# A hybrid encoder's mixers: large elementwise work leaves GpSimd for VectorE and ScalarE

## The chip, the cores and the metric

The kernel runs on one core of a Trainium2 chip. A core has TensorE (PE, matrix products into PSUM), VectorE (DVE), ScalarE (ACT, functions and scaled copies), GpSimd (POOL) and SyncE (SP), which here only issues transfers. Each engine works through its own queue in order; semaphores order them against each other. The metric is the device time of one execution in microseconds.

## The reference, cut to what matters

Two layers over 256 tokens of 1024 features, all in float32. Each layer is: half a SwiGLU feed-forward step, a mixer, half a SwiGLU step.

```python
x = x + 0.5 * swiglu_ffn(x, ffn1_norm[l], ffn1_wi[l], ffn1_wo[l])
h = rmsnorm(x, mix_norm[l])
(a_q, a_k, a_v, sc_u, c_qlat, c_kvlat, c_krope, lru_u, gate_lin) = jnp.split(h @ w_in[l], split_idx, axis=-1)
o_a = gqa_mixer(...)          # 8 heads, softmax over 256 keys
o_b = shortconv_mixer(...)    # B * conv3(C * x)
o_c = mla_mixer(...)          # 8 heads from low-rank latents
o_d = rglru_mixer(...)        # gelu(gate) * (recurrence forwards + backwards)
y = jnp.einsum('bsnc,ncd->bsnd', branches, w_branch[l])
x = x + jnp.sum(sigmoid(gate_lin) * y, axis=2) @ w_out[l]
x = x + 0.5 * swiglu_ffn(x, ffn2_norm[l], ffn2_wi[l], ffn2_wo[l])
```

In the recurrence the decay is a = exp(-y) with y = 8 softplus(-lambda) r, and the input is scaled by sqrt(1 - a^2).

## The kernel before, in words

Every matrix product is made in float32r with both operands split in two parts that sum to them: `mm` (lines 208 to 212) issues high x high, low x high and high x low. So each weight that comes from memory is split on the chip: `Weights.split` (line 100) copies a unit of up to 1024 columns into a high part on ScalarE (line 110) and takes the difference, the low part, on VectorE (line 113). In some stretches every `share`-th low part is made on GpSimd (line 112): every fourth one from the mixer's first slot to the slot of the recurrence's output, every one from the last head's slot until the output projection. `AHEAD` = 2 units are split ahead of the one in use; four buffers hold high parts and four low parts.

A feed-forward step (`ffn`, line 382) is a long run of products of 128 features x 256 tokens with little else.

The mixer (line 475) first makes the latents and the queries, keys and values token by token, then runs a list of slots (line 905). A slot has an attention head or none, products that keep PE fed, and other work. For a head, `scores` and `exps` (line 445) make the scores, the row maxima on VectorE (line 448), a bias (line 450) and on ScalarE the exponentials with their row sums (line 454). `normalise` (line 459) takes the reciprocal and scales the probabilities on VectorE (line 462). One or two slots later `probs_t` (line 464) transposes them on PE and splits the result (`split`, lines 217 and 218), and `head_values` (line 952) multiplies them with the values (line 966), copies one half to the other half's partitions (line 968), adds (line 969) and splits the sum.

Beside this run: the scaling of the latents by their norm on VectorE (`lat_scale`, line 548); the width-4 and width-3 convolutions, all taps on VectorE (lines 649 and 652, 762 and 765); the recurrence's gates, decay (`lru_decay`, line 695: argument on VectorE, one exponential and one tanh of 1024 columns on ScalarE), roots (`lru_root`, line 705: a square root on ScalarE, then three GpSimd products or sums for each direction), scans on VectorE (line 719), closing sum and product on GpSimd (lines 722 and 723); the gelu (lines 665 to 672); the squares of the MLA norms on GpSimd (lines 803 and 808); and for each branch the gated up-projection, whose running sum is on GpSimd (line 880). The last branch's sum is on VectorE (lines 1008 and 1009), followed by the split of the merged features (line 1011, whose parts are `mgh` and `mgl`) and the output projection `pw`.

The order of the instructions on each engine isn't that of the program: a planner of the language lays it out when the kernel is built, with a simulated timeline of its own, so a change of engines can move instructions that the diff doesn't touch.

Of the kernel before, what the change touches and what calls it, by code (L numbers as in the profile page):

```python
# [15 lines left out]
DEPTH = 2  # L16
D = 1024
T = 256
# [10 lines left out]
# columns of the combined input projection  # L29
# [11 lines left out]
# per-layer columns of the packed per-channel parameters  # L41
# [7 lines left out]
# per-layer columns of the packed row vectors, then the rotary tables  # L49
# [7 lines left out]
# the first transfers of weights hold one unit each; so many of them go ahead of the constants  # L57
FIRST = 7
EARLY = 10
# GQA heads between a head's scores and its use  # L60
LAG = 2
# opening work in order: operand pair of x's tile k (k), split of the next weights (-1), square of tile k (10 + k)
# [3 lines left out]
class Weights:  # L66
    """Streams the weights in the order of their use and hands out each piece as two float32r
    parts that sum to it. Without the packed array it only records that order."""
# [3 lines left out]
    def __init__(self, nc, flat=None, order=None, raw_pool=None, hi_pool=None, lo_pool=None):  # L72
        self.nc, self.flat = nc, flat
        self.raw_pool, self.hi_pool, self.lo_pool = raw_pool, hi_pool, lo_pool
        self.recording = order is None
        self.order = [] if self.recording else order
        self.chunks = [] if self.recording else chunks_of(order)
        self.spare = None  # where the first transfers go
        self.share, self.n = 0, 0  # every share-th low part on GpSimd
        self.ci, self.off, self.loaded, self.ready, self.now = 0, 0, [], [], []  # L80
# [19 lines left out]
    def split(self):  # L100
# [10 lines left out]
        self.n += 1  # L111
        eng = self.nc.gpsimd if self.share and self.n % self.share == 0 else self.nc.vector
        b = eng.tensor_tensor(lo[:, :w], src, hi[:, :w].bitcast(F32), op=ALU.subtract)  # L113
# [20 lines left out]
def chunks_of(order):  # L134
    """Pieces grouped into split units of at most UNIT columns, those into transfers of MAXC."""
# [20 lines left out]
class Null:  # L156
    """Stands for every object of a trace that only records the order of the weights."""
# [18 lines left out]
def hybrid_encoder(ctx: ExitStack, tc: tile.TileContext, xT, par, rows, ident_d, flat, out, order=None):  # L176
# [31 lines left out]
    def mm(out, lhs, rhs, start, stop):  # L208
        """out (+)= lhs.T @ rhs, each operand a (high, low) pair of float32r."""
# [4 lines left out]
    def split(hi, lo, src, scale=None):  # L214
        """hi + lo = src (times a per-partition or constant scale)."""
# [9 lines left out]
    ones = const.tile([P, 1], F32, name="ones")  # L225
    V.memset(ones, 1.0)
    # brings ScalarE's function table on chip before the first data
# [24 lines left out]
    chp = const.tile([P, DEPTH, 8], F32, name="chp")  # L252
    hba = const.tile([P, DEPTH, 16], F32, name="hba")
    gqk = const.tile([P, DEPTH], F32, name="gqk")

    def prepare_parameters():
# [10 lines left out]
        # 4 softplus(-lam): log1p(exp(-|lam|)) by its series in z / (2 + z)  # L267
# [14 lines left out]
        V.tensor_scalar(chp, acc, 2.0, None, op0=ALU.mult)  # L282

# [3 lines left out]
    def rope_tables(l):  # L287
        """cos * gain and sin * (gain of the partner) for GQA q, k and MLA q, k."""
# [16 lines left out]
    def rope_swap(tmp, src, tabs, b, heads, d):  # L305
        """tmp = sin terms: the partners of src [P, heads, d] times sin * gain."""
# [12 lines left out]
    class Norm:  # L319
        """Operand pairs of x * gain as x's tiles become final, and the 1/rms they still lack."""  # L320
# [21 lines left out]
        def scale(self):  # L342
            """1/rms of every token, on the tokens' partitions."""
# [10 lines left out]
        def scale_rows(self):  # L354
            """The same as a row on all partitions."""
# [12 lines left out]
    def group(dst, name, l, kts, c0, pairs):  # L368
        """dst [128 features, T] = sum over k of W[k, c0:c0+128].T @ pairs[k]."""
# [3 lines left out]
    def groups(dsts, name, l, kts, c0s, pairs, late):  # L373
        """The same for several targets; the last `late` operands are left to the end."""
# [70 lines left out]
    def exps(pS, scl):  # L445
        """scl: per block [P, 1] scale of the scores."""
# [12 lines left out]
    def normalise(pe, sm):  # L459
        V.reciprocal(sm, sm)  # L460
        for b in range(2):
            V.tensor_scalar(pe[:, b, :], pe[:, b, :], sm[:, b : b + 1], None, op0=ALU.mult)
# [12 lines left out]
    def mixer(l, nrm, tabs, nxt):  # L475
        def tok_group(c0, width, wname, pairs, kts):
            """Token-major products of one column range, one bank per token block."""
# [15 lines left out]
        # latents, queries, keys and values, token-major  # L493
# [6 lines left out]
        # the function table of the attention and the gates, ahead of their need  # L500
# [4 lines left out]
        # fully normalised operand for the feature-major projections  # L505
# [19 lines left out]
        # norms of the latents  # L525
# [19 lines left out]
        def lat_scale():  # L545
            for b in range(2):
                for i, (o, w) in enumerate(spans):
                    V.tensor_scalar(lat[b][:, o : o + w], lat[b][:, o : o + w], lrs[:, b, i : i + 1], None, op0=ALU.mult)

        # transposed latents  # L550
# [13 lines left out]
        # GQA norms, rotary and operands  # L564
# [68 lines left out]
        # RG-LRU: width-4 convolution, gates, recurrences in both directions  # L633
# [11 lines left out]
        def lru_taps(p):  # L645
            for n in (2 * p, 2 * p + 1):
                src = lr["pad"][:, n, :]
                acc = lr["xc"][:, n * T : (n + 1) * T]
                V.tensor_scalar(acc, src[:, 0:T], col(l, O_LCW + n), col(l, O_LCB + n), op0=ALU.mult, op1=ALU.add)
# [11 lines left out]
        def gelu_gate():  # L661
            """2 gelu(gate) = gate * (1 + tanh(sqrt(2/pi) * (gate + 0.044715 gate^3)))."""
# [3 lines left out]
            V.tensor_scalar(gl, gl, 0.044715, 1.0, op0=ALU.mult, op1=ALU.add)  # L666
            G.tensor_tensor(gl, gl, lg, op=ALU.mult)

        def gelu_tanh():
            lg, gl = lr["g"], lr["gelu"]  # L670
            A.activation(gl, gl, AF.Tanh, scale=math.sqrt(2.0 / math.pi))
# [23 lines left out]
        def lru_decay(d):  # L695
            """a = exp(-y) and tanh(y / 2) for y = 8 softplus(-lambda) r; i * x."""
            r3 = th_r[d].rearrange("p (n t) -> p n t", t=T)
            c3 = chp[:, l, d * 4 : d * 4 + 4].unsqueeze(2).to_broadcast([P, 4, T])
            V.scalar_tensor_tensor(r3, r3, 1.0, c3, op0=ALU.add, op1=ALU.mult)
            dec[d] = m4("dec")  # L700
            A.activation(dec[d], th_r[d], AF.Exp, scale=-2.0)
            A.activation(th_r[d], th_r[d], AF.Tanh)
            V.scalar_tensor_tensor(th_i[d], th_i[d], 1.0, lr["xc"], op0=ALU.add, op1=ALU.mult)

        def lru_root():
            """sqrt(1 - a^2) = (1 + a) sqrt(tanh(y / 2)), quartered for i's and gelu's tanh forms."""
            A.activation(lr["r"], lr["r"], AF.Sqrt, scale=0.0625)
            for d in range(2):
                G.tensor_tensor(th_i[d], th_i[d], th_r[d], op=ALU.mult)
                G.tensor_tensor(th_r[d], th_i[d], dec[d], op=ALU.mult)  # L710
                G.tensor_tensor(th_i[d], th_i[d], th_r[d], op=ALU.add)
# [9 lines left out]
        def lru_add():  # L721
            G.tensor_tensor(th_r[0], th_r[0], th_r[1], op=ALU.add)
            G.tensor_tensor(th_r[0], th_r[0], lr["gelu"], op=ALU.mult)
# [14 lines left out]
        # short convolution  # L738
# [6 lines left out]
        def sc_x(p, pb):  # L745
# [12 lines left out]
            for j in range(2):  # L758
# [3 lines left out]
                V.tensor_scalar(acc, src[:, 0:T], col(l, O_SCW + n), col(l, O_SCB + n), op0=ALU.mult, op1=ALU.add)  # L762
# [10 lines left out]
        # MLA: up-projections, norms, rotary and operands  # L773
# [25 lines left out]
        def mla_square(which):  # L799
            for b in range(2):  # L800
                if which == 0:
                    sq = m3("sqm", cols=768)
                    G.tensor_tensor(sq, ml["qm"][b], ml["qm"][b], op=ALU.mult)
                    sq = sq.rearrange("p (h d) -> p h d", d=MD)
                else:
                    sq = m3("sqm", cols=512).rearrange("p (h d) -> p h d", d=HD)
                    kn = ml["kv3"][b][:, :, 0:64]
                    G.tensor_tensor(sq, kn, kn, op=ALU.mult)
# [36 lines left out]
        def mla_transpose(g, which):  # L845
            """Feature-major operand pair of heads 4g..4g+3."""
# [12 lines left out]
        # branch gates, up-projections and their gated sum  # L859
# [10 lines left out]
        def up(b, p, name):  # L870
            def done(p, pb):
# [6 lines left out]
                else:  # L878
                    V.scalar_tensor_tensor(t, t, 1.0, pb, op0=ALU.add, op1=ALU.mult)
                    G.tensor_tensor(mgp[p], mgp[p], t, op=ALU.add)  # L880
# [266 lines left out]
```

## Time and profile before

| what | us |
|---|---|
| median of 3 runs | 1418.28 (1417.96 to 1418.98) |
| span of the profiled execution, first to last instruction | 1416.7 |
| PE busy in that span | 1377.8 |
| VectorE busy | 999.4 |
| ScalarE busy | 746.0 |
| GpSimd busy | 247.0 |

For the profiled execution no time beside its span is listed; the median is 1.6 us above the span. The busy time of PE is the time in which a matmul or transposition was running, by modelled ends, so it contains slow ones too. The mixers lie between about 200 and 515 us and between about 905 and 1215 us; the rest is feed-forward.

### The profile page before, as it was taken

How to read it: one execution, taken by the hardware profiler on the slowest of the kernel's cores; microseconds unless marked ns; L12 is line 12 of the kernel's file. 1: busy time of each engine (PE TensorE's matmuls, PEld its weight loads, DVE VectorE, ACT ScalarE, POOL GpSimd, SP SyncE). 2: the span in 40 equal slices, each digit the busy share in tenths (PEclk: the TensorE clock that was granted, in tenths of full speed). 3: DMA queues.
4: the chain of work that ended last, by engine and by line, in shares of the span. 5: the costliest groups of instructions: out<-in, count | busy, mean ns of one | idle time of the engine just before them, and what ended most of it. 6: DMA issues, size and time to landing. Idle time of an engine off the chain costs nothing.

```text
span 1416.7 us, 26507 instructions
## 1 busy us (share of the span) xinstructions
PE 1377.8 (97%) x11184; PEld 1364.5 (96%) x11184; DVE 999.4 (71%) x1334; ACT 746.0 (53%) x1104; POOL 247.0 (17%) x199
## 2 busy tenths in 40 slices
PE   8999999997999999999999999999989999999999
PEld 8999999897899999999999999999889999999999
DVE  6666558989877676666566665599899777666653
ACT  6444447584556555444444444566745564554432
POOL 3200004329610400000000000032456104000000
PEclk9999999999999999999999999999999999999999
DMA  7555545433454355555555555444325534555552
GB/s 280 184 187 191 183 152 202 149 120 129 155 179 149 120 180 188 193 184 179 183 180 194 188 179 180 163 176 165 118 108 183 197 127 149 179 179 181 186 206 76
DMA packets 35831, 240.81 MB, mean 170 GB/s; under 512 B 3968, under 2 KB 5376, under 8 KB 9472
## 3 DMA queue, kind: packets, MB, share of 16 engines
q1 hardware_dynamic: 35712, 239.12, 47.6%
q8 instruction: 87, 1.43, 0.4%
q14 instruction: 32, 0.26, 0.1%
HBM read 238.06 MB, written 1.05 MB: 169 GB/s over the span
## 4 chain that ended last, share of the span: by engine, by line
PE 88%; DVE 5%; issue 2%; POOL 2%; ACT 1%; DMA 0%; SPq 0%; DVEq 0%; POOLq 0%; ACTq 0%
PE pg L211 6%; PE pu L211 6%; PE pg L212 6%; PE pg L210 6%; PE pu L212 6%; PE pu L210 6%; PE po L211 6%; PE po L210 6%; PE po L212 6%; PE pgt L210 4%; PE pgt L211 3%; PE pgt L212 3%; PE pa L211 2%; PE pa L212 2%; PE pa L210 2%
## 5 line engine op out<-in xcount | busy, mean ns | idle before, releaser
L110 ACT CAST hi<-raw 128x1024 fp32r<-128x1024 f32 (+4 forms) x459 | 474.2, 1035 | 500.5 <-PE po L211 117.0
L113 DVE TENSOR_TENSOR lo<-raw,hi 128x1024 fp32r<-128x1024 f32 (+4 forms) x428 | 539.5, 1261 | 276.1 <-ACT hi L110 274.5
L210 PE MATMUL pg<-xh,hi 128*128 128x256 f32 x704 | 199.0, 283 | 6.1 <-ACT hi L110 6.1
L211 PE MATMUL pg<-xl,hi 128*128 128x256 f32 x704 | 199.5, 283 | 0.0
L212 PE MATMUL pg<-xh,lo 128*128 128x256 f32 x704 | 199.2, 283 | 0.0
L211 PE MATMUL pu<-xl,hi 128*128 128x256 f32 x704 | 198.8, 282 | 0.0
L210 PE MATMUL pu<-xh,hi 128*128 128x256 f32 x704 | 198.4, 282 | 0.0
L212 PE MATMUL pu<-xh,lo 128*128 128x256 f32 x704 | 198.3, 282 | 0.0
L211 PE MATMUL po<-hl,hi 128*128 128x256 f32 x704 | 198.0, 281 | 0.0
L212 PE MATMUL po<-hh,lo 128*128 128x256 f32 x704 | 197.7, 281 | 0.0
L210 PE MATMUL po<-hh,hi 128*128 128x256 f32 x704 | 197.7, 281 | 0.0
L210 PE MATMUL pgt<-xnh,hi 128*128 128x256 f32 x512 | 146.4, 286 | 0.0
L212 PE MATMUL pgt<-xnh,lo 128*128 128x256 f32 x512 | 145.0, 283 | 0.7 <-DVE lo L113 0.7
L211 PE MATMUL pgt<-xnl,hi 128*128 128x256 f32 x512 | 145.5, 284 | 0.0
L210 PEld LDWEIGHTS pg<-xh,hi 128*128 128x128 f32 x704 | 133.8, 190 | 6.4 <-ACT hi L110 6.4
L212 PEld LDWEIGHTS pg<-xh,lo 128*128 128x128 f32 x704 | 133.8, 190 | 0.2 <-DVE lo L113 0.2
L211 PEld LDWEIGHTS pg<-xl,hi 128*128 128x128 f32 x704 | 133.8, 190 | 0.0
L212 PEld LDWEIGHTS pu<-xh,lo 128*128 128x128 f32 x704 | 133.1, 189 | 0.2 <-DVE lo L113 0.2
L211 PEld LDWEIGHTS pu<-xl,hi 128*128 128x128 f32 x704 | 133.2, 189 | 0.0
L210 PEld LDWEIGHTS pu<-xh,hi 128*128 128x128 f32 x704 | 133.0, 189 | 0.0
L211 PEld LDWEIGHTS po<-hl,hi 128*128 128x128 f32 x704 | 132.7, 188 | 0.0
L212 PEld LDWEIGHTS po<-hh,lo 128*128 128x128 f32 x704 | 132.6, 188 | 0.0
(301 smaller groups left out, 3052.7 us busy)
## 6 DMA issues: line engine op xcount, KB each, us to landing
raw<-weights SPq DMA_DIRECT2D x205, 1024.0 KB, 4.8
raw<-weights SPq DMA_DIRECT2D x9, 768.0 KB, 4.3
raw<-weights SPq DMA_DIRECT2D x4, 896.0 KB, 4.6
raw<-weights SPq DMA_DIRECT2D x3, 1008.0 KB, 4.7
raw<-weights SPq DMA_DIRECT2D x5, 512.0 KB, 8.0
out<-xg SPq DMA_DIRECT2D x8, 128.0 KB, 2.1
raw<-weights SPq DMA_DIRECT2D x1, 1016.0 KB, 4.8
raw<-weights SPq DMA_DIRECT2D x1, 968.0 KB, 4.6
```

What stands on the lines that cost most here:

```text
L110: a = self.nc.scalar.copy(hi[:, :w], src)
L113: b = eng.tensor_tensor(lo[:, :w], src, hi[:, :w].bitcast(F32), op=ALU.subtract)
L210: TE.matmul(out, lhs[0], rhs[0], start=start, stop=False)
L211: TE.matmul(out, lhs[0], rhs[1], start=False, stop=False)
L212: TE.matmul(out, lhs[1], rhs[0], start=False, stop=stop)
```

## The change

Low parts of weights are made on VectorE only (`share` is gone). Probabilities and latents are scaled on ScalarE. The first tap of both convolutions, with its bias, is made on ScalarE. In the decay the addition of 1 and the factor of each channel move into scale and bias of ScalarE's exponential and tanh, which are now issued for each 256 columns; a second small constant `chn` holds the factor of the exponential. The gelu's polynomial is one VectorE instruction in place of one on VectorE and one on GpSimd. The roots are two VectorE instructions for each direction in place of three on GpSimd. Closing sum and product of the recurrence and the gated sums move to VectorE, the squares of the MLA norms to ScalarE. Comments are removed as well, which the cut leaves out.

```diff
-        self.n += 1
-        eng = self.nc.gpsimd if self.share and self.n % self.share == 0 else self.nc.vector
-        b = eng.tensor_tensor(lo[:, :w], src, hi[:, :w].bitcast(F32), op=ALU.subtract)
+        b = self.nc.vector.tensor_tensor(lo[:, :w], src, hi[:, :w].bitcast(F32), op=ALU.subtract)
...
+        V.tensor_scalar(chn, acc, -4.0, None, op0=ALU.mult)
...
-            V.tensor_scalar(pe[:, b, :], pe[:, b, :], sm[:, b : b + 1], None, op0=ALU.mult)
+            A.activation(pe[:, b, :], pe[:, b, :], AF.Copy, scale=sm[:, b : b + 1])
...
-                    V.tensor_scalar(lat[b][:, o : o + w], lat[b][:, o : o + w], lrs[:, b, i : i + 1], None, op0=ALU.mult)
+                    A.activation(lat[b][:, o : o + w], lat[b][:, o : o + w], AF.Copy, scale=lrs[:, b, i : i + 1])
...
-                V.tensor_scalar(acc, src[:, 0:T], col(l, O_LCW + n), col(l, O_LCB + n), op0=ALU.mult, op1=ALU.add)
+                A.activation(acc, src[:, 0:T], AF.Identity, scale=col(l, O_LCW + n), bias=col(l, O_LCB + n))
...
-            V.tensor_scalar(gl, gl, 0.044715, 1.0, op0=ALU.mult, op1=ALU.add)
-            G.tensor_tensor(gl, gl, lg, op=ALU.mult)
+            V.scalar_tensor_tensor(gl, gl, 1.0 / 0.044715, lg, op0=ALU.add, op1=ALU.mult)
...
-            A.activation(gl, gl, AF.Tanh, scale=math.sqrt(2.0 / math.pi))
+            A.activation(gl, gl, AF.Tanh, scale=0.044715 * math.sqrt(2.0 / math.pi))
...
-            V.scalar_tensor_tensor(r3, r3, 1.0, c3, op0=ALU.add, op1=ALU.mult)
             dec[d] = m4("dec")
-            A.activation(dec[d], th_r[d], AF.Exp, scale=-2.0)
-            A.activation(th_r[d], th_r[d], AF.Tanh)
+            for n in range(4):
+                sl, c = slice(n * T, (n + 1) * T), slice(d * 4 + n, d * 4 + n + 1)
+                A.activation(dec[d][:, sl], th_r[d][:, sl], AF.Exp, scale=chn[:, l, c], bias=chn[:, l, c])
+                A.activation(th_r[d][:, sl], th_r[d][:, sl], AF.Tanh, scale=chp[:, l, c], bias=chp[:, l, c])
...
-                G.tensor_tensor(th_i[d], th_i[d], th_r[d], op=ALU.mult)
-                G.tensor_tensor(th_r[d], th_i[d], dec[d], op=ALU.mult)
-                G.tensor_tensor(th_i[d], th_i[d], th_r[d], op=ALU.add)
+                V.scalar_tensor_tensor(th_r[d], dec[d], 1.0, th_r[d], op0=ALU.add, op1=ALU.mult)
+                V.tensor_tensor(th_i[d], th_i[d], th_r[d], op=ALU.mult)
...
-            G.tensor_tensor(th_r[0], th_r[0], th_r[1], op=ALU.add)
-            G.tensor_tensor(th_r[0], th_r[0], lr["gelu"], op=ALU.mult)
+            V.tensor_tensor(th_r[0], th_r[0], th_r[1], op=ALU.add)
+            V.tensor_tensor(th_r[0], th_r[0], lr["gelu"], op=ALU.mult)
...
-                V.tensor_scalar(acc, src[:, 0:T], col(l, O_SCW + n), col(l, O_SCB + n), op0=ALU.mult, op1=ALU.add)
+                A.activation(acc, src[:, 0:T], AF.Identity, scale=col(l, O_SCW + n), bias=col(l, O_SCB + n))
...
-                    G.tensor_tensor(sq, ml["qm"][b], ml["qm"][b], op=ALU.mult)
+                    A.square(sq, ml["qm"][b])
...
-                    G.tensor_tensor(sq, kn, kn, op=ALU.mult)
+                    A.square(sq, kn)
...
-                    G.tensor_tensor(mgp[p], mgp[p], t, op=ALU.add)
+                    V.tensor_tensor(mgp[p], mgp[p], t, op=ALU.add)
```

The calls of `share` in the slots and after the last branch are removed.

## Rows read from the trace of the kernel before

**Rows 1.** The page's first part: busy time, share of the span and instructions of each engine.

```profile
PE 1377.8 (97%) x11184; PEld 1364.5 (96%) x11184; DVE 999.4 (71%) x1334; ACT 746.0 (53%) x1104; POOL 247.0 (17%) x199
```

**Rows 2.** Windows: the stretch, its length, busy time (and instructions) of PE, weight loads, VectorE, ScalarE and GpSimd, the granted clock, the share and rate of transfers. A piece of the first mixer, the first mixer, the two feed-forward steps between, the second mixer.

```profile
300.00:375.00 75.00, 63.09 (x454) 59.88 (x454) 66.98 (x80) 45.07 (x75) 52.29 (x27) 0.93 0.34 119
222.00:515.00 293.00, 276.44 (x2184) 269.86 (x2183) 242.12 (x345) 171.56 (x293) 114.76 (x71) 0.98 0.42 150
515.00:923.00 408.00, 408.00 (x3400) 408.00 (x3400) 256.27 (x313) 198.53 (x257) 4.82 (x10) 1.00 0.52 184
923.00:1215.00 292.00, 278.89 (x2194) 273.13 (x2193) 244.66 (x352) 175.80 (x297) 101.72 (x54) 0.98 0.43 152
```

**Rows 3.** PE's waits over the whole span: which instructions waited for which, us in total, times, the longest.

```profile
PE pov L966 <- DVE pl L218: 13.0, 4, 4.5
PE pov L966 <- ACT ph L217: 6.4, 3, 3.1
PE pg L210 <- ACT hi L110: 6.1, 2, 4.6
PE pw L211 <- DVE mgl L221: 4.7, 2, 2.4
PE pa L211 <- POOL lo L113: 1.4, 1, 1.4
PE pkT L615 <- DVE ro L605: 1.3, 1, 1.3
```

**Rows 4.** Windows of 5 us in the columns of rows 2: beside the attention stalls (325, 330, 355, 1030, 1055 us) and behind the output projection's (500, 1200 us).

```profile
325.00:330.00 5.00, 1.49 (x7) 1.49 (x8) 4.93 (x6) 0.00 (x0) 5.00 (x3) 0.53 0.47 161
330.00:335.00 5.00, 5.00 (x33) 4.54 (x33) 4.83 (x7) 3.36 (x7) 3.35 (x1) 0.78 0.00 2
355.00:360.00 5.00, 3.62 (x14) 3.62 (x15) 3.44 (x6) 0.65 (x2) 0.12 (x1) 0.66 0.28 85
500.00:505.00 5.00, 5.00 (x33) 5.00 (x33) 2.66 (x6) 1.07 (x3) 0.00 (x0) 0.72 0.51 180
1030.00:1035.00 5.00, 3.44 (x17) 3.44 (x18) 4.76 (x8) 1.57 (x5) 3.01 (x2) 0.69 0.01 3
1055.00:1060.00 5.00, 4.69 (x19) 4.69 (x20) 4.97 (x5) 3.55 (x6) 2.72 (x2) 0.66 0.21 85
1200.00:1205.00 5.00, 4.99 (x23) 4.99 (x24) 3.19 (x7) 0.83 (x2) 0.00 (x0) 0.50 0.51 200
```

**Rows 5.** VectorE's timeline in the first mixer: start, duration (of all `xN` together), line, instruction, tiles, in brackets the idle time ahead of it.

```profile
304.30 0.61 DVE L462 TENSOR_SCALAR pe<-pe,sm 128x256 f32<-128x256 f32 x2
...
314.53 2.58 DVE L113 TENSOR_TENSOR lo<-raw,hi 128x1024 fp32r<-128x1024 f32 x1 [3.41 <-ACT hi L110]
...
317.24 4.69 DVE L462 TENSOR_SCALAR pe<-pe,sm 128x256 f32<-128x256 f32 x2
...
322.42 2.83 DVE L113 TENSOR_TENSOR lo<-raw,hi 128x1024 fp32r<-128x1024 f32 x1
325.17 2.57 DVE L218 TENSOR_TENSOR oal<-o,oah 128x256 fp32r<-128x256 f32 x1
327.77 0.69 DVE L218 TENSOR_TENSOR pl<-pT,ph 128x512 fp32r<-128x512 f32 x1
...
350.45 4.82 DVE L462 TENSOR_SCALAR pe<-pe,sm 128x256 f32<-128x256 f32 x2
```

**Rows 6.** GpSimd's timeline in the same stretch, in the same columns.

```profile
313.63 5.74 POOL L709 TENSOR_TENSOR thi<-thi,thr 128x1024 f32<-128x1024 f32 x2 [12.76 <-ACT thr L707]
319.30 2.48 POOL L710 TENSOR_TENSOR thr<-thi,dec 128x1024 f32<-128x1024 f32 x1
321.74 2.42 POOL L113 TENSOR_TENSOR lo<-raw,hi 128x1024 fp32r<-128x1024 f32 x1
...
327.40 5.95 POOL L711 TENSOR_TENSOR thi<-thi,thr 128x1024 f32<-128x1024 f32 x2
```

**Rows 7.** VectorE's instructions in groups of one line, shape and operation: count, busy us, mean ns, idle time before. In this order: the feed-forward stretch from 540 to 920 us (one row), the first mixer from 222 to 515 us (two rows), the second from 923 to 1215 us (three rows).

```profile
L113 DVE TENSOR_TENSOR lo<-raw,hi 128x1024 fp32r<-128x1024 f32 x124 | 151.7, 1224 | 104.1 <-ACT hi L110 104.1
...
L113 DVE TENSOR_TENSOR lo<-raw,hi 128x1024 fp32r<-128x1024 f32 x65 | 87.5, 1348 | 19.7 <-ACT hi L110 18.7
L462 DVE TENSOR_SCALAR pe<-pe,sm 128x256 f32<-128x256 f32 x32 | 20.8, 691 | 0.6
...
L113 DVE TENSOR_TENSOR lo<-raw,hi 128x1024 fp32r<-128x1024 f32 x65 | 90.0, 1389 | 21.3 <-ACT hi L110 20.7
L462 DVE TENSOR_SCALAR pe<-pe,sm 128x256 f32<-128x256 f32 x32 | 12.4, 431 | 0.6
L1009 DVE TENSOR_TENSOR mg<-mg,th 128x256 f32<-128x256 f32 x8 | 7.1, 909 | 0.0
```

**Rows 8.** GpSimd's groups over the whole span, in the columns of rows 7: low parts of weights, gated sums.

```profile
L113 POOL TENSOR_TENSOR lo<-raw,hi 128x1024 fp32r<-128x1024 f32 x28 | 70.1, 2506 | 165.5 <-ACT hi L110 164.9 <-PE pT L469 0.6
L880 POOL TENSOR_TENSOR mg<-mg,th 128x512 f32<-128x512 f32 x16 | 21.8, 1362 | 74.9 <-DVE th L879 74.9
```

**Rows 9.** ScalarE's groups over the whole span, in the columns of rows 7: the residual's scaling into its high part, the residual's square.

```profile
L220 ACT ACTIVATE xh<-xg,prm 128x256 fp32r<-128x256 f32 x40 | 20.2, 505 | 2.9 <-DVE xg L435 2.7 <-DVE xg L1021 0.2
...
L336 ACT ACTIVATE sq<-xg 128x256 f32<-128x256 f32 x42 | 16.4, 403 | 0.0
```

**Rows 10.** ScalarE's waits over the whole span, in the columns of rows 3.

```profile
ACT pe L454 <- DVE nb L450: 32.6, 11, 5.8
```

More of the change, by code (lines that the diff above doesn't have):

```diff
@@ L78, in __init__ @@
         self.spare = None
-        self.share, self.n = 0, 0
         self.ci, self.off, self.loaded, self.ready, self.now = 0, 0, [], [], []
@@ L252, in hybrid_encoder @@
     chp = const.tile([P, DEPTH, 8], F32, name="chp")
+    chn = const.tile([P, DEPTH, 8], F32, name="chn")
     hba = const.tile([P, DEPTH, 16], F32, name="hba")
@@ L695, in lru_decay @@
         def lru_decay(d):
-            r3 = th_r[d].rearrange("p (n t) -> p n t", t=T)
-            c3 = chp[:, l, d * 4 : d * 4 + 4].unsqueeze(2).to_broadcast([P, 4, T])
-            V.scalar_tensor_tensor(r3, r3, 1.0, c3, op0=ALU.add, op1=ALU.mult)
             dec[d] = m4("dec")
-            A.activation(dec[d], th_r[d], AF.Exp, scale=-2.0)
-            A.activation(th_r[d], th_r[d], AF.Tanh)
+            for n in range(4):
+                sl, c = slice(n * T, (n + 1) * T), slice(d * 4 + n, d * 4 + n + 1)
+                A.activation(dec[d][:, sl], th_r[d][:, sl], AF.Exp, scale=chn[:, l, c], bias=chn[:, l, c])
+                A.activation(th_r[d][:, sl], th_r[d][:, sl], AF.Tanh, scale=chp[:, l, c], bias=chp[:, l, c])
             V.scalar_tensor_tensor(th_i[d], th_i[d], 1.0, lr["xc"], op0=ALU.add, op1=ALU.mult)
@@ L899, in call @@
             return lambda: f(*args)
-        def share(n):
-            return lambda: setattr(W, "share", n)
         slots = [
-            (None, [proj("pxb", C_XB, 0, lru_conv)], [share(4), lat_norms, gqa_norms, lat_scale]),
+            (None, [proj("pxb", C_XB, 0, lru_conv)], [lat_norms, gqa_norms, lat_scale]),
             (None, [proj("pxb", C_XB, 1, lru_conv)], [lat_transpose, call(gqa_rotate, 0), call(gqa_rotate, 1), call(lru_taps, 0)]),
@@ L920, in mixer @@
             (None, [gate(1, 3), up(1, 3, "ob"), call(mla_up, 1, "kvup")], [lru_out, call(mla_square, 0)]),
-            (None, [gate(3, 0), up(3, 0, "od")], [share(0), call(mla_sum, 0), call(mla_swap, 0), call(mla_square, 1)]),
+            (None, [gate(3, 0), up(3, 0, "od")], [call(mla_sum, 0), call(mla_swap, 0), call(mla_square, 1)]),
             (None, [gate(3, 1), up(3, 1, "od")], [call(mla_sum, 1), call(mla_query, 0), call(mla_swap, 1), mla_values]),
@@ L931, in mixer @@
             (14, [gate(2, 2)], []),
-            (15, [gate(2, 3), share(1)], []),
+            (15, [gate(2, 3)], []),
             (None, [up(0, 2, "oa"), up(0, 3, "oa")], []),
@@ L1011, in mixer @@
             split(*merged[n], m, scale=0.5)
-        W.share = 0
         pws = [bank("pw")[:, :T] for _ in range(2)]
```

## The prediction

> **What bounds the kernel now.** I read the page's busy line first: PE is busy 1377.8 of 1416.7 us [rows 1]. So at most 38.9 us are idle time of PE, and no engine but PE can be the limit on the average; what the other engines can change is only when PE stands still. The windows by stage come next [rows 2]: in the feed-forward stretch from 515 to 923 us PE is busy 408.00 of 408.00 us with 3400 matmuls, 0.120 us each, and there the change touches nothing. The two mixers show the idle time: 293.0 - 276.4 = 16.6 us in the first and 292.0 - 278.9 = 13.1 us in the second, 29.7 us together. The rest (about 9 us) is the opening and the last store.
>
> PE's waits say where this lies [rows 3]. The values' matmuls of the attention heads wait 13.0 us for the low part of the transposed probabilities (VectorE) and 6.4 us for the high part (ScalarE); a low part of weights made on GpSimd costs 1.4 us: 20.8 us in the attention stretches (group A). The output projection waits 4.7 us for the merged branches (group B). The keys' transposition waits 1.3 us (group C).
>
> Behind the long waits the clock is down [rows 4]. Granted shares of 0.53, 0.78, 0.66, 0.69 and 0.66 stand in five windows of 5 us beside the attention stalls, 0.72 and 0.50 after the output projection's. A share below 1 is a mixture of the two levels, 1.2 and 2.4 GHz. What this cost is (1 - share) x PE busy: 0.70 + 1.10 + 1.23 + 1.07 + 1.59 = 5.7 us beside A, 1.40 + 2.50 = 3.9 us behind B.
>
> Why VectorE is late there is seen by laying its timeline over GpSimd's [rows 5, 6]. Two probability scalings take 0.61 us together at 304.30 us, and 4.69 us at 317.24 us; a low part of weights takes 2.58 and 2.83 us, a 128x256 low part 2.57 us. In just this time GpSimd runs without a gap from 313.6 to 333.4 us: the recurrence's products and one low part. The scalings end at 321.93 us, just after the GpSimd product that runs to 321.78; the low part begun at 322.42 ends at 325.25, 1.1 us (its own time) after the GpSimd low part that runs to 324.16. In the same time the probabilities' low part at 327.77 us, which reads one operand from PSUM, takes its normal 0.69 us beside a GpSimd product. I read this as two engines that can't both read two SBUF operands at once: one stands until the other's instruction is over. At 350.45 us the scalings again take 4.82 us. Behind both places stands a stall of PE of over 4 us (the longest of rows 3), because scaled probabilities, their transposition and the values' product follow each other.
>
> **The change, part by part.** *Off GpSimd:* the low parts of weights (28 of 1024 columns at 2.51 us, and three shorter ones), the gated sums (16 at 1.36 us) [rows 8], the recurrence's products (12, 2.5 to 3.0 us each [rows 6]), and 14 closing steps, gate products and squares of 1.4 to 3 us (an estimate from these rows by size). That is about 82 + 22 + 34 + 30 = 168 of 247 us [rows 1]. What is left is small: powers of row sums, the rotary swaps, memsets.
>
> *Onto VectorE:* an unhindered 1024-column instruction with two SBUF inputs takes 1.22 us [rows 7], one of 512 columns 0.69 us [rows 5]. Low parts of weights 31 x 1.22 = 38 us, gated sums 16 x 0.69 = 11 us, the roots' products 8 x 1.22 = 9.8 us (12 GpSimd instructions become 8 here), the two closing steps 4 x 1.22 = 4.9 us, the gate's fused step about 2 x 0.6 = 1.1 us: 65 us. *Off VectorE:* 64 probability scalings at 0.61 / 2 = 0.31 us [rows 5] = 20 us, the decay's argument 4 x 1.22 = 4.9 us, first taps and latents about 24 x 0.35 = 8.4 us (estimates from the scaling's 0.31 us): 33 us. Net + 32 us, 16 us for each mixer.
>
> Against it stands what VectorE loses now by standing. Its low parts of weights take 1348 and 1389 ns in the mixers and 1224 ns in the feed-forward stretch: 65 x 0.124 = 8.1 and 65 x 0.165 = 10.7 us. The scalings take 20.8 and 12.4 us where 32 x 0.31 = 9.9 us are due: 10.9 and 2.5 us. Eight sums of the second mixer's end take 7.1 us instead of 8 x 0.37 = 3.0: 4.1 us [rows 7]. So at least 19.0 and 17.3 us of standing go, against 16 us of work that comes: VectorE's sum hardly moves, 242 to 245 us a mixer [rows 2]. The gain isn't a lighter VectorE but that its instructions keep to their short times, and a chain of three of them no longer takes 10 us.
>
> *Onto ScalarE:* 64 scalings of 128x256, with a factor for each partition. The nearest rows are a square without such a factor, 403 ns, and the residual's scaling with one, 505 ns [rows 9]; I take the second, 64 x 0.505 = 32 us. 16 first taps at the same price 8 us, 8 latent scalings about 4 us, the decay in 32 pieces instead of 8 whole instructions about 5 us, eight squares of the MLA norms about 6 us (estimates from the same two rows by size): 55 us, some 27 us a mixer. ScalarE is at 171.6 and 175.8 of 293 us [rows 2], so this lies beside PE's work. On this the Trainium skill speaks against the move: "ScalarE: Activation LUTs", section "What ACT_TABLE_LOAD costs", says that an instruction without a pointer takes 186 ns and 0.833 ns an element, and that each pointer operand adds some 93 ns. By it a scaling would take an estimated 493 ns, 60% more than VectorE's 0.31 us; the trace agrees (505 ns). By the pointerless price the 64 would be 26 us; neither reaches PE.
>
> *A wait that is added:* on ScalarE the scaling stands behind VectorE's reciprocal of the row sums, which itself waits for ScalarE's exponentials. Queued behind it are the high parts of weights, and PE waits for those. What covers it is the lead of the weights: two units of 8 pieces with 3 matmuls each, 2 x 24 x 0.120 = 5.8 us. ScalarE already stands 32.6 us behind VectorE for the scores' bias, up to 5.8 us at a time [rows 10], and the only wait of PE for high parts of weights, 6.1 us [rows 3], is the opening's. I price the new wait at 0, with 32 x 1.5 us as the upper bound if the cover is gone (below).
>
> *The sum.* Group A 20.8 + 5.7 us, B 4.7 + 3.9 us, C 1.3 us: 36.4 us if everything goes. What stays: from 300 to 375 us VectorE is busy 67.0 of 75 us [rows 2]. Take off the stretch of rows 5: (2.58 - 1.22) + (4.69 - 0.61) + (2.83 - 1.22) + (2.57 - 0.41) + (4.82 - 0.61) = 13.4 us and five pairs of scalings, 3 us; add four low parts of weights 4.9, root products 4.9, closing steps 2.4, gate 0.6 = 12.8 us: 63 us of work, where PE's own need is 63.1 us less its slow-clock loss, about 60 us. VectorE is still full there, so a chain can still come late; I keep a third of A: 7 us idle and 2 us of clock. For B: the two sums and low parts of rows like those above get short, but two low parts of weights come onto VectorE in the same 10 us; I keep 1 us of idle and 1 us of clock. Gain 36.4 - 11 = 25.4 us. The profiled execution's span is 1416.7 us, 1.6 us below the median of 1418.28 us; the span's prediction is 1391.3 us, with the same 1.6 us around it 1393 us.
>
> **The rivals.** *Half comes back (1404 to 1414 us).* VectorE at 100% between 300 and 375 us, and at 1010 to 1060 us likewise, makes the attention chain late as before: only C, B and a third of A go, 1.3 + 6.6 + 8.8 = 16.7 us less, or 1401.6 us, and with new short waits for low parts of weights (31 more of them queue on VectorE, at an estimated 0.3 us each: 9 us) 1411 us. For it: the 63 against 60 us above. Against it: the standing I could take off came from a few rows alone, so the 63 us are an upper value.
>
> *No difference (within 0.2%).* The standing of VectorE isn't due to GpSimd's SBUF reads, so the times stay. Against it: the ends in rows 5 follow those in rows 6. The Trainium skill has this as a rule ("SBUF — State Buffer", section "Who interferes with whom"): a VectorE instruction with two SBUF inputs, or in a mode that uses both ports, and a GpSimd instruction that reads SBUF exclude each other, and the one that comes second stands for the whole of the first. By that rule this case wouldn't arise, and the trace agrees; the chance stays at 0.08 because the order of instructions on each engine is laid out anew by the planner when engines change, which no row of before shows.
>
> *Slower (1430 us).* The added wait decides. It stands in ScalarE's queue once a head. If VectorE's queue ahead of the reciprocal is over 5.8 us long when ScalarE gets there, the high parts behind come late; at an estimated 1.5 us of stall in each of the 32 heads this is 48 us, against the 36.4 us: 1418.3 - 36.4 + 48 = 1430 us. For it: ScalarE's waits for VectorE reach that length already [rows 10], where VectorE itself stood behind GpSimd. Against it: just this standing goes.
>
> **How the numbers follow.** The forecast (1380 to 1403 us) 0.63; half comes back 0.17; no difference 0.08; slower 0.12. About 0.2%, 2.8 us, is what a measurement of this kernel can tell from no change. So faster 0.80, same 0.08, slower 0.12. The low end is all of the 36.4 us gone, 1382 us, and some 2 us of PE's shorter waits that I gave no row; the high end reaches into the second case and leaves about 0.2 above it: 1412 us.
>
> **What would show it.** GpSimd's busy time near 80 us (247 - 168); PE's waits for the two parts of the probabilities under 8 us in total; no low part of weights over 1.5 us from 310 to 360 us; ScalarE's scaling at 0.40 to 0.51 us; the clock windows behind the attention stalls at 1.00. I am wrong if VectorE's instructions stay long without GpSimd, or if PE's waits turn to the high parts of weights behind ScalarE's scaling, or to low parts queued on VectorE.

## The result, and the profile after

The changed kernel takes 1385.96 us (median of 4 runs, 1385.48 to 1386.98) beside 1418.4 us for the kernel before: a ratio of 0.9771, 95% interval 0.9757 to 0.9785. The forecast was 1393 us with 1380 to 1412 as its range.

The page's first part (answers to [rows 1]):

```profile
PE 1367.8 (99%) x11184; PEld 1356.3 (98%) x11184; DVE 939.7 (68%) x1302; ACT 798.0 (58%) x1224; POOL 90.6 (7%) x126
```

Read it against PE first. The span went from 1416.7 to 1385.2 us, 31.5 us. PE has the same 11184 matmuls and is busy 10.0 us less. Of this 7.4 us is clock: (1 - share) x busy time, summed over all windows of 5 us, was 10.6 us and is 3.1 us. Its idle time fell from 38.9 to 17.4 us, 21.5 us. Then VectorE: it received work and is busy 59.7 us less. Windows by stage and of 5 us, in the columns of [rows 2] and [rows 4]:

```profile
300.00:375.00 75.00, 73.70 (x568) 71.02 (x567) 64.54 (x97) 60.80 (x102) 16.51 (x12) 1.00 0.45 161
222.00:505.00 283.00, 279.53 (x2247) 274.32 (x2246) 220.78 (x346) 202.65 (x361) 33.02 (x35) 0.99 0.46 161
505.00:910.00 405.00, 405.00 (x3364) 405.00 (x3362) 251.99 (x302) 197.09 (x256) 4.82 (x10) 1.00 0.52 183
910.00:1190.00 280.00, 275.52 (x2220) 270.25 (x2220) 216.07 (x341) 200.85 (x356) 26.90 (x17) 0.99 0.45 160
325.00:330.00 5.00, 5.00 (x38) 4.44 (x37) 5.00 (x9) 4.59 (x10) 0.00 (x0) 1.00 0.13 18
330.00:335.00 5.00, 5.00 (x43) 5.00 (x43) 5.00 (x10) 3.12 (x6) 0.00 (x0) 1.00 0.48 195
485.00:490.00 5.00, 5.00 (x32) 5.00 (x31) 2.08 (x5) 0.42 (x1) 0.00 (x0) 0.66 0.47 197
1170.00:1175.00 5.00, 4.17 (x22) 3.97 (x21) 2.32 (x7) 1.18 (x3) 0.00 (x0) 0.66 0.26 108
```

The gain lies in the mixers; the feed-forward stretch is as before. From 300 to 375 us PE ran 454 matmuls before and runs 568 now, while VectorE is about as busy (66.98 and 64.54 us) and GpSimd has dropped from 52.29 to 16.51 us. The clock is at 1.00 where the attention stalls had been, and at 0.66 in two windows only, both behind the output projection.

PE's waits (answers to [rows 3]):

```profile
PE pg L207 <- ACT hi L109: 5.8, 2, 4.8
PE pw L209 <- DVE lo L110: 2.4, 2, 1.3
PE pS L207 <- ACT qTh L214: 1.7, 2, 1.0
PE pa L208 <- DVE lo L110: 1.2, 1, 1.2
PE pov L959 <- ACT ph L214: 1.0, 1, 1.0
PE pw L208 <- DVE mgl L218: 1.0, 2, 0.8
...
PE pw L207 <- ACT mgh L217: 0.3, 1, 0.3
```

The 13.0 us for the probabilities' low part are gone, the 6.4 us for their high part are 1.0. What the output projection waits for has changed its name from the merged features to a low part of its weights (L110), and is hardly less: 2.4 + 1.0 + 0.3 us (L209, L208, L207) where there were 4.7 us for low parts and 0.6 us for a high part.

VectorE's timeline in the stretch of [rows 5]:

```profile
321.10 2.36 DVE L706 SCALAR_TENSOR_TENSOR thr<-dec,thr 128x1024 f32<-128x1024 f32 x2 [0.81 <-ACT thr L704]
323.49 0.69 DVE L215 TENSOR_TENSOR pl<-pT,ph 128x512 fp32r<-128x512 f32 x1
324.10 1.22 DVE L707 TENSOR_TENSOR thi<-thi,thr 128x1024 f32<-128x1024 f32 x1
325.23 1.22 DVE L110 TENSOR_TENSOR lo<-raw,hi 128x1024 fp32r<-128x1024 f32 x1
326.37 1.22 DVE L707 TENSOR_TENSOR thi<-thi,thr 128x1024 f32<-128x1024 f32 x1
327.50 0.42 DVE L215 TENSOR_TENSOR oal<-o,oah 128x256 fp32r<-128x256 f32 x1
```

A low part of weights takes 1.22 us here (2.58 and 2.83 before) and the 128x256 low part 0.42 us (2.57). The roots' products, 2.5 to 3.3 us each on GpSimd, take 1.2 us each. Groups of the whole span, ScalarE's scaling of the probabilities (answers to [rows 9]):

```profile
L461 ACT ACTIVATE pe<-pe,sm 128x256 f32<-128x256 f32 x64 | 29.4, 510 | 1.9 <-DVE sm L459 1.9
```

### The profile page after: what moved, and what is told of

It is laid out like the page before. It is cut to its first block, busy times and chain, and to the rows that moved or that the text cites. A ratio compares the mean times of both kernels' runs of the same rounds, so it can differ in the third digit from the quotient of the medians.

```text
span 1385.2 us, 26443 instructions
## 1 busy us (share of the span) xinstructions
PE 1367.8 (99%) x11184; PEld 1356.3 (98%) x11184; DVE 939.7 (68%) x1302; ACT 798.0 (58%) x1224; POOL 90.6 (7%) x126
## 5 line engine op out<-in xcount | busy, mean ns | idle before, releaser
L110 DVE TENSOR_TENSOR lo<-raw,hi 128x1024 fp32r<-128x1024 f32 (+4 forms) x459 | 553.3, 1208 | 294.4 <-ACT hi L109 293.5
L207 PE MATMUL pg<-xh,hi 128*128 128x256 f32 x704 | 199.0, 283 | 5.8 <-ACT hi L109 5.8
L208 PE MATMUL pg<-xl,hi 128*128 128x256 f32 x704 | 199.5, 283 | 0.0
L209 PE MATMUL pg<-xh,lo 128*128 128x256 f32 x704 | 199.3, 283 | 0.0
L209 PE MATMUL pu<-xh,lo 128*128 128x256 f32 x704 | 198.3, 282 | 0.5 <-DVE lo L110 0.5
L208 PE MATMUL pu<-xl,hi 128*128 128x256 f32 x704 | 198.6, 282 | 0.0
L207 PE MATMUL pu<-xh,hi 128*128 128x256 f32 x704 | 198.5, 282 | 0.0
L208 PE MATMUL po<-hl,hi 128*128 128x256 f32 x704 | 197.9, 281 | 0.0
L209 PE MATMUL po<-hh,lo 128*128 128x256 f32 x704 | 197.4, 280 | 0.0
L207 PE MATMUL po<-hh,hi 128*128 128x256 f32 x704 | 197.3, 280 | 0.0
L207 PE MATMUL pgt<-xnh,hi 128*128 128x256 f32 x512 | 145.7, 285 | 0.0
L208 PE MATMUL pgt<-xnl,hi 128*128 128x256 f32 x512 | 144.6, 282 | 0.0
L209 PE MATMUL pgt<-xnh,lo 128*128 128x256 f32 x512 | 144.0, 281 | 0.0
L207 PEld LDWEIGHTS pg<-xh,hi 128*128 128x128 f32 x704 | 133.7, 190 | 6.1 <-ACT hi L109 6.1
L209 PEld LDWEIGHTS pg<-xh,lo 128*128 128x128 f32 x704 | 133.8, 190 | 0.3 <-DVE lo L110 0.2
L208 PEld LDWEIGHTS pg<-xl,hi 128*128 128x128 f32 x704 | 133.8, 190 | 0.0
L209 PEld LDWEIGHTS pu<-xh,lo 128*128 128x128 f32 x704 | 133.1, 189 | 0.7 <-DVE lo L110 0.7
L208 PEld LDWEIGHTS pu<-xl,hi 128*128 128x128 f32 x704 | 133.1, 189 | 0.0
L207 PEld LDWEIGHTS pu<-xh,hi 128*128 128x128 f32 x704 | 133.0, 189 | 0.0
L207 PEld LDWEIGHTS po<-hh,hi 128*128 128x128 f32 x704 | 132.6, 188 | 0.0
L209 PEld LDWEIGHTS po<-hh,lo 128*128 128x128 f32 x704 | 132.5, 188 | 0.0
```

What stands on the lines that cost most here:

```text
L110: b = self.nc.vector.tensor_tensor(lo[:, :w], src, hi[:, :w].bitcast(F32), op=ALU.subtract)
L207: TE.matmul(out, lhs[0], rhs[0], start=start, stop=False)
L208: TE.matmul(out, lhs[0], rhs[1], start=False, stop=False)
L209: TE.matmul(out, lhs[1], rhs[0], start=False, stop=stop)
```

## The experiments

Two theories. *Exclusion*: while GpSimd reads SBUF, VectorE's instructions with SBUF operands stand; what is gained is that GpSimd is quiet, and what ScalarE took over matters little. *Load*: VectorE and its chain were full, and the gain is what ScalarE took off them; then work that only moves from GpSimd to VectorE should cost time. A third reading, that GpSimd's slow instructions were simply links of the chain that PE waits for, is put to j_read below.

**p_low.** The kernel before with every low part of weights on VectorE.

```diff
-        self.n += 1
-        eng = self.nc.gpsimd if self.share and self.n % self.share == 0 else self.nc.vector
-        b = eng.tensor_tensor(lo[:, :w], src, hi[:, :w].bitcast(F32), op=ALU.subtract)
+        b = self.nc.vector.tensor_tensor(lo[:, :w], src, hi[:, :w].bitcast(F32), op=ALU.subtract)
```

> The kernel before with one part of the change: every low part of weights on VectorE. Exclusion theory (VectorE stood while GpSimd instructions read SBUF; taking these off GpSimd is the gain): the output projection's waits and clock loss (4.7 + 3.9 us), the keys' wait (1.3) and the wait for a low part made on GpSimd (1.4) go, the recurrence's products still hold VectorE: 1403 to 1409 us. Load theory (VectorE is relieved by what moves to ScalarE; work that leaves GpSimd only burdens it): 38 us more on VectorE and nothing relieved, 1418 to 1430 us.

Measured: 1406.82 us, ratio 0.9914 (0.99 to 0.9929). Page and PE's waits:

```profile
PE 1373.9 (98%) x11184; PEld 1361.5 (97%) x11184; DVE 992.0 (71%) x1365; ACT 747.2 (53%) x1104; POOL 171.8 (12%) x168
```

```profile
PE pov L964 <- DVE pl L216: 15.5, 4, 7.1
...
PE pw L210 <- DVE lo L111: 2.3, 2, 1.3
...
PE pw L209 <- DVE mgl L219: 0.9, 2, 0.7
```

VectorE got 31 instructions more, about 38 us of work, and is busy 7.4 us *less*. The wait for the merged features falls from 4.7 to 0.9 us, but at the same place PE now waits 2.3 us for low parts of weights, and behind the second mixer's projection the clock is down as before (3.1 us of loss). The waits for the keys and for a low part from GpSimd, 1.3 and 1.4 us, are gone. The attention stall stays (15.5 us): in its stretch the recurrence's products still run on GpSimd. So the time is in the range of the exclusion, but not all the terms of that range came true: of the projection's 4.7 + 3.9 us less than half went.

**p_prod.** The kernel before with the recurrence's products, its closing steps, the gelu and the gated sums on VectorE and the squares on ScalarE.

```diff
-                G.tensor_tensor(th_i[d], th_i[d], th_r[d], op=ALU.mult)
-                G.tensor_tensor(th_r[d], th_i[d], dec[d], op=ALU.mult)
-                G.tensor_tensor(th_i[d], th_i[d], th_r[d], op=ALU.add)
+                V.scalar_tensor_tensor(th_r[d], dec[d], 1.0, th_r[d], op0=ALU.add, op1=ALU.mult)
+                V.tensor_tensor(th_i[d], th_i[d], th_r[d], op=ALU.mult)
...
-                    G.tensor_tensor(mgp[p], mgp[p], t, op=ALU.add)
+                    V.tensor_tensor(mgp[p], mgp[p], t, op=ALU.add)
```

> The kernel before with another part alone: the recurrence's products and closing steps, the gelu's product and the gated sums on VectorE, the squares of the MLA norms on ScalarE; low parts of weights stay shared with GpSimd, scalings stay on VectorE. Exclusion theory: the stalls behind 323 us and at 1026 to 1031 us go with their clock loss (5.3 + 6.4 + 3 us) and about half of those behind 350 and 1052 us: 1398 to 1406 us. Load theory: 27 us more on VectorE, 1418 to 1428 us.

Measured: 1396.2 us, ratio 0.9831 (0.9814 to 0.9847), somewhat better than either expectation. PE's waits:

```profile
PE pw L211 <- DVE mgl L221: 4.6, 2, 2.4
PE pov L964 <- DVE pl L218: 4.2, 2, 2.2
```

The other half: the attention stall is down to 4.2 us and the wait for the merged features stays at 4.6 us; the last low parts are still made on GpSimd there. Each of the two waits goes with the GpSimd work of its own stretch, but at the projection a wait for VectorE's low parts of weights takes part of its place.

**p_act.** The kernel before with only ScalarE's part: scalings of probabilities and latents, first taps, the decay's argument.

```diff
-            V.tensor_scalar(pe[:, b, :], pe[:, b, :], sm[:, b : b + 1], None, op0=ALU.mult)
+            A.activation(pe[:, b, :], pe[:, b, :], AF.Copy, scale=sm[:, b : b + 1])
...
-            A.activation(dec[d], th_r[d], AF.Exp, scale=-2.0)
+                A.activation(dec[d][:, sl], th_r[d][:, sl], AF.Exp, scale=chn[:, l, c], bias=chn[:, l, c])
```

> The kernel before with the last part alone: the scalings of probabilities and latents, first taps and the decay's argument on ScalarE; GpSimd keeps all its work. Exclusion theory: the scalings that took 4.69, 4.82 and 3.22 us leave VectorE's chain, but low parts of weights and of the heads' sums are still held: 1406 to 1414 us. Load theory: this is where the gain is, 1386 to 1396 us.

Measured: 1411.24 us, ratio 0.9944 (0.9929 to 0.9959). PE's waits:

```profile
PE pov L967 <- ACT ph L217: 7.6, 4, 3.2
...
PE pov L967 <- DVE pl L218: 2.8, 3, 1.3
```

VectorE is 42 us lighter (957.4 us) and only 7.4 us of time come of it. The chain is shorter by the scalings that had stood behind GpSimd; the rest of the stall stays.

**u_act.** Both GpSimd parts without ScalarE's: the edits of p_low and p_prod together.

> The two GpSimd parts together, without the move to ScalarE (scalings, first taps and decay's argument stay on VectorE, some 33 us more there than in the changed kernel). Exclusion theory: nothing holds the scalings any more (0.31 us each), most of the gain stays: 1386 to 1396 us. Load theory: VectorE carries 65 us more than before, 1418 us or more.

Measured: 1386.73 us, ratio 0.9775 (0.976 to 0.9789): the whole gain, with VectorE at 969.6 us. VectorE's scalings of the first mixer, which [rows 7] had at 691 ns:

```profile
L460 DVE TENSOR_SCALAR pe<-pe,sm 128x256 f32<-128x256 f32 x32 | 9.8, 349 | 0.4
```

So once GpSimd is quiet they cost VectorE half of it. PE still waits for them:

```profile
PE pT L467 <- DVE pe L460: 3.5, 3, 1.8
```

The changed kernel doesn't have this wait, but others of about the same sum (1.7 us for `qTh`, 1.2 us for a low part, 1.0 us for `ph`, above), and the two times are the same. The load theory falls here: it gave 1418 us or more.

**u_norm and u_scal.** The changed kernel with the probabilities' scalings back on VectorE (u_norm), and u_act with these scalings alone on ScalarE (u_scal).

```diff
-            A.activation(pe[:, b, :], pe[:, b, :], AF.Copy, scale=sm[:, b : b + 1])
+            V.tensor_scalar(pe[:, b, :], pe[:, b, :], sm[:, b : b + 1], None, op0=ALU.mult)
```

> The changed kernel with one part undone: the 64 scalings of the probabilities back on VectorE. Exclusion theory: each takes about 0.31 us there, nothing holds it, and ScalarE has 29 us less: 1385 to 1391 us. Load theory: 20 us come back onto VectorE, full between 300 and 375 us: 1396 us or more.

> Both GpSimd parts, and of ScalarE's part the scalings of the probabilities only; first taps, latents and decay argument stay on VectorE. With the runs without any of it (1386.7 us), with all of it (1386.0 us) and with all but the scalings (1391.3 us) this closes the square. If the scalings on ScalarE are worth 5.3 us by VectorE's load, they bring 1386.7 down to 1381 to 1383 us here. If the 5.3 us are an order laid out less well in one version, the scalings bring nothing by themselves: 1385 to 1389 us.

Measured: u_norm 1391.3 us (0.981, 0.9794 to 0.9826), u_scal 1389.69 us (0.9796, 0.9783 to 0.981), 0.3 and 0.7 us above the upper end of the range that goes without an effect of load. With nothing of ScalarE's part it is 1386.7 us, with one piece 1389.7, with the other 1391.3, with both 1386.0: no sum of two effects. Both middle versions show one new stall of PE, at about 1030 us; PE's waits of u_norm, then of u_scal:

```profile
PE pov L959 <- ACT ph L214: 4.0, 2, 3.1
```

```profile
PE pov L962 <- ACT ph L215: 3.1, 1, 3.1
```

A stall that two different versions share and that neither the lighter nor the heavier neighbour has looks like a matter of how the planner lays out the instructions around this head. Instructions do move there: of the changed kernel's 1052 VectorE instructions between 200 and 1250 us at most 965 stand in the same order in u_norm, whose edit touches none of them. That the order makes the stall was not shown, since no run holds it fixed; what is shown is that moving the scalings is worth between -5 and +3 us by the rest of the version, and that VectorE's load doesn't decide it: its busy time is 969.6, 957.8, 952.0 and 939.7 us where the times are 1386.7, 1391.3, 1389.7 and 1386.0 us.

**j_read and j_write.** The changed kernel with idle work on GpSimd in each mixer, beside the roots: twelve 128x512 products that read two SBUF tiles, or one such product and 36 memsets that only write. Their result is read by nobody.

```diff
+            for _ in range(12):
+                G.tensor_tensor(idle, dec[1][:, :512], lr["g"][:, :512], op=ALU.mult)
```

```diff
+            G.tensor_tensor(idle, dec[1][:, :512], lr["g"][:, :512], op=ALU.mult)
+            for _ in range(36):
+                G.memset(idle, 0.0)
```

> The changed kernel with 12 idle GpSimd products of 128x512 in each mixer at the place of the roots, whose result nobody reads (both operands from SBUF, some 16 us of GpSimd in a mixer). No chain gets longer by them. Exclusion theory: VectorE's instructions with two SBUF operands stand beside them, stalls of the values' matmuls come back: 1392 to 1402 us. Theory that GpSimd's slow instructions were simply links of the chain PE waited for: 1386 us, unchanged.

> As the one before, but after a first product the idle GpSimd work is 36 memsets in each mixer, which read nothing. Exclusion theory in the form that the reads of SBUF exclude each other: VectorE's two-operand instructions keep their times, 1385 to 1388 us. If any GpSimd work beside VectorE costs: as the one before.

Measured: j_read 1397.34 us (0.9853, 0.9839 to 0.9868), j_write 1385.79 us (0.9772, 0.9758 to 0.9787). GpSimd's timeline of j_read, then VectorE's:

```profile
308.92 23.67 POOL L707 TENSOR_TENSOR idle<-dec,lg 128x512 bf16<-128x512 f32 x12 [52.37 <-ACT dec L699]
```

```profile
321.27 3.46 DVE L709 SCALAR_TENSOR_TENSOR thr<-dec,thr 128x1024 f32<-128x1024 f32 x2 [0.78 <-ACT thr L705]
324.77 0.69 DVE L215 TENSOR_TENSOR pl<-pT,ph 128x512 fp32r<-128x512 f32 x1
...
326.89 2.30 DVE L110 TENSOR_TENSOR lo<-raw,hi 128x1024 fp32r<-128x1024 f32 x1
329.12 2.32 DVE L710 TENSOR_TENSOR thi<-thi,thr 128x1024 f32<-128x1024 f32 x1
331.36 1.51 DVE L215 TENSOR_TENSOR oal<-o,oah 128x256 fp32r<-128x256 f32 x1
```

The same two of j_write:

```profile
309.59 20.92 POOL L708 MEMSET idle<- 128x512 bf16 x36
```

```profile
320.59 2.36 DVE L710 SCALAR_TENSOR_TENSOR thr<-dec,thr 128x1024 f32<-128x1024 f32 x2 [0.78 <-ACT thr L705]
...
324.72 1.22 DVE L110 TENSOR_TENSOR lo<-raw,hi 128x1024 fp32r<-128x1024 f32 x1
...
326.99 0.42 DVE L215 TENSOR_TENSOR oal<-o,oah 128x256 fp32r<-128x256 f32 x1
```

This is the cleanest pair. GpSimd is about equally busy in both (133.7 and 131.1 us), nothing waits for its idle work, and between 200 and 1250 us VectorE's instructions stand in the changed kernel's order but for a handful (1042 of 1046 in j_read, 1047 of 1051 in j_write). With reads the low part takes 2.30 us instead of 1.22 and the 128x256 one 1.51 instead of 0.42, and 11.4 us are lost; with writes alone nothing is. The low part that takes one operand from PSUM (L215 `pl`) keeps its 0.69 us beside GpSimd's reads. PE's waits of j_read:

```profile
PE pa L208 <- DVE lo L110: 4.9, 3, 2.8
PE pup L209 <- DVE lo L110: 2.5, 1, 2.5
...
PE pov L962 <- DVE pl L215: 1.0, 2, 0.6
```

The stall comes back at another place than I expected: low parts of weights are late (1.2 and 0.4 us in the changed kernel), while the values' matmuls wait for VectorE only 1.0 us. The reading that GpSimd's slow instructions were links of the chain gave 1386 us here and can't explain the 11.4 us; in the kernel before, PE waited for GpSimd itself only the 1.4 us of [rows 3]. No run splits the whole 32.4 us further.

**t_late and t_four, u_four.** For what stays at the output projection: it starts with four groups of 128 columns in place of two, and leaves the last three merged features to the end (t_late) or the last four (t_four; u_four is the same in u_act).

```diff
-        pws = [bank("pw")[:, :T] for _ in range(2)]
-        groups(pws, "wout", l, range(KT), (0, P), merged, 2)
+        pws = [bank("pw")[:, :T] for _ in range(4)]
+        groups(pws, "wout", l, range(KT), (0, P, 2 * P, 3 * P), merged, 3)
...
-            if n < 2:
+            if n < 4:
```

> An attempt at a faster version: the output projection starts with four column groups and leaves their last three operands to the end (two and two in the changed kernel), so that PE has other products while VectorE finishes the merged branches. If the rest there (3.7 us of waits and some 3 us of clock loss) is a matter of the order of products: 1379 to 1382 us. If VectorE's sum of work there is the bound: 1386 us.

> The changed kernel, whose output projection starts with four column groups instead of two and leaves the last four merged features to the end instead of the last two. In the version with four groups and three features left, TensorE still waited 3.7 us for low parts of merged features (the fifth one, ready at 483.9 us) at the granted clock of 1.00. If that is because the fifth feature is asked for too early, here only the first four are needed in the first pass, the last of them is ready at 480.3 us and the first pass lasts 4 x 12 x 0.117 = 5.6 us, to 485.9 us: waits of about 0 to 1 us, 1380 to 1382.5 us. If VectorE's work of this stage as a whole is the bound (the eighth low part is ready at 487.0 us), the wait only moves to the second pass and the time stays at 1383 to 1385 us.

> The same start of the output projection in the version that has both GpSimd parts and leaves scalings, first taps and decay argument on VectorE. If the move to ScalarE is worth nothing once GpSimd is quiet, this takes the same time as the run with the change's ScalarE part, within 2 us of it (1380 to 1384 us). If the move relieves VectorE at the output projection, this one stays at least 2 us above it.

Measured: t_late 1384.17 us (0.9761, 0.9747 to 0.9776), t_four 1385.13 us (0.9765, 0.9752 to 0.9779), u_four 1386.44 us (0.9774, 0.9761 to 0.9787). t_late's waits of PE and the windows behind the projection:

```profile
PE pw L208 <- DVE mgl L218: 3.7, 2, 2.3
```

```profile
485.00:490.00 5.00, 5.00 (x45) 5.00 (x44) 3.09 (x7) 2.53 (x3) 0.00 (x0) 1.00 0.43 180
1170.00:1175.00 5.00, 5.00 (x45) 5.00 (x44) 1.90 (x3) 2.60 (x3) 0.00 (x0) 1.00 0.00 0
```

The wait has only changed its name again, from the weights' low part back to the merged features, 3.7 us in all three versions with four groups. In t_late the clock behind it stays at 1.00, which (1 - 0.66) x (5.00 + 4.17) = 3.1 us had been lost to in the changed kernel; its median is 1.8 us lower, about 0.13%, less than I call a difference, and lies between the two times that I gave. Why the clock stays up there behind waits of the same sum, no run shows. t_four has the same wait:

```profile
484.67 0.39 PE L208 MATMUL pw<-mgl,hi 128*128 128x256 f32 x1 [1.40 <-DVE mgl L218]
```

It doesn't test what it was built for. PE comes to this wait after 16 of the projection's matmuls, as in t_late, where a first pass over four features in four groups has 48: the order in front of the wait is not the one that the expectation reckoned with. So whether a feature is asked for too early stays open. VectorE's work in these 10 us, sums and low parts without a gap, fits as well, but wasn't tried by making that work smaller. u_four lies 1.3 us above t_four, within the 2 us in which ScalarE's part was to be worth nothing, though both are above the times that I gave.

## Why the prediction was right, and where its sizes were off

*The bound and the mechanism.* PE as the bound, its idle time in three groups, the clock behind the stalls, and GpSimd's SBUF reads as the reason for VectorE's lateness: each stood up. p_prod took away most of group A and left B; p_low took C and the wait for the merged features, but not all of B; j_read brought the standing back with VectorE's order all but unchanged, and j_write excluded GpSimd's mere activity. The Trainium skill's rule, "SBUF — State Buffer", section "Who interferes with whom", that a two-input VectorE instruction and a GpSimd instruction reading SBUF exclude each other, agrees with j_read (2.30 for 1.22 us). GpSimd is at times the one that stands: the 24 products of j_read took 1854 ns on average, the single ones of j_write 1298 ns.

*Group A, the mis-sized term.* I kept a third of it, 7 us of idle time and 2 us of clock, because I reckoned VectorE's work at 63 us where PE needs 60. What remains is 1.0 us for `ph` and 1.2 us for a low part, and no clock: 2.2 of 26.5 us. The reckoning took the standing off only in the rows that I had in front of me: VectorE is busy 64.54 us there now, but while PE runs 568 matmuls, which by proportion is an estimated 52 us for the 454 before. By the prediction's own terms VectorE should be at 999.4 + 65 - 33 = 1031 us less the standing; it is at 939.7, so some 92 us of standing went, where I had counted 36. The step "VectorE's sum hardly moves, 242 to 245 us a mixer" is wrong with it: 220.8 and 216.1 us.

*Group B, too small a rest.* I kept 1 + 1 us; 2.4 + 1.0 + 0.3 = 3.7 us of idle time and the 3.1 us of clock stay, 6.8 of 8.6 us (0.3 us of it is the wait for a high part, 0.6 us before, which the 8.6 left out). I named the reason (two low parts of weights come onto VectorE in the same 10 us) and priced it too low: the merged features came earlier, and the weights' low part became the one that is late. One of my signs of being wrong, PE's waits turning to low parts queued on VectorE, thus came true on a small scale: 2.4 us here, 1.2 us in the attention stretch.

*Group C* went as forecast: no wait for the keys' rotary remains.

*The sum.* Gone of the priced groups: 24.3 (A) + 1.8 (B) + 1.3 (C) = 27.4 us, against the 25.4 I forecast. That these lie so near is in part luck, two errors of opposite sign: A's rest was 6.8 us too large, B's 4.8 us too small. The other 4.1 of the 31.5 us had no row in the prediction. About 1 us is slow clock in windows that I hadn't listed, 0.6 us other idle time of PE; for the rest, 2.5 us of PE's busy time that the clock doesn't explain, I have no row. The rival "half comes back" was given as 1404 to 1414 us although its own sum began at 1401.6 us; the measured time is below both.

*What moved where.* GpSimd is at 90.6 us (forecast: near 80). ScalarE's scaling at 510 ns was priced at 505, and its sum rose by 52 us (55). The Trainium skill's "ScalarE: Activation LUTs", section "What ACT_TABLE_LOAD costs", gave an estimated 493 ns with the pointer's surcharge; the trace agrees better with that than with the pointerless 403 ns. The added wait of ScalarE for the reciprocal, priced at 0, measures 1.9 us over the whole span and delays nothing of PE's. That disposes of the rival "slower"; its premise, a long VectorE queue ahead of the reciprocal, went with the standing, as I had argued against it.

*What I credited wrongly.* I entered the moves to ScalarE as relief of VectorE, 33 us that balance 65. u_act shows that this part brings nothing beside the others (1386.7 and 1386.0 us), while alone it brings 7.4 us: it was a way round GpSimd, and once GpSimd is quiet there is nothing to go round.

## What to carry to other kernels

Work given to an engine that looks idle isn't free if it blocks the busy one: compare the mean duration of one instruction form in a quiet stretch and in the crowded one, over all forms and not just the worst, before you count what the second engine saves. Test parts of a change together as well as alone: the alone-gains 11.9, 22.5 and 7.4 us add up to 41.8, and all three give 32.4. When a stall's name changes and its length doesn't, look for what both names share before you reorder its consumers.

## What the hardware showed that I had not expected

GpSimd's writes, which I had left open, cost VectorE nothing: 36 memsets in a row over 20.92 us, and VectorE's instructions beside them keep 1.22 and 0.42 us to the hundredth.

VectorE's loss was spread far wider than the instructions that looked slow: some 92 us, or 9% of its busy time, for 156 us that GpSimd worked more (247.0 against 90.6 us). Form by form the two traces say much the same: the forms that both kernels have on VectorE lost about 70 us by their means, the scalings 64 x (561 - 310) ns = 16 us. Even the scores' bias, 2 columns wide, took 630 ns on average and takes 155 ns.
